# Adaptive average pooling: the last wait and its semaphore's clear, on GpSimd instead of SP

## The chip, the cores and the metric

The kernel runs on one core of one Trainium2 chip. A time is in device microseconds, lower being better, and comes from single executions of the program; the median of several is given with the lowest and highest. The profile is one such execution, recorded by the hardware profiler; its span goes from the first to the last instruction of the program.

Engines are named as in the profile: DVE is VectorE, ACT is ScalarE, POOL is GpSimd, SP is SyncE (no compute, it issues transfers and waits), PE is TensorE (idle in this kernel). A "q" behind a name (SPq, POOLq) is that engine's sequencer, which waits, signals and issues DMAs.

## The reference

```python
def setup_inputs():
    batch, channels, length = 32, 256, 4096
    output_size = 256
    ...

def reference(x, output_size):
    for i in range(output_size):
        start = int(i * length / output_size)
        end = int((i + 1) * length / output_size)
        result[:, :, i] = np.mean(x[:, :, start:end], axis=-1)
```

The input is 32 x 256 x 4096 float32, the output 32 x 256 x 256 float32. As 4096 is a multiple of 256, each output is the mean of its own 16 neighbours: 134 MB are read and 8.4 MB written.

## The kernel before

Batch and channel together give 8192 rows of 4096 values. They are spread over 128 partitions, four rows of a partition to a tile (`R = 4`), so a tile is 128 x 16384 float32 and there are 16 of them. The first 14 tiles belong to one set of rows and write into the buffer `res_many`; the last two, the tail, into `res_few`. Each of the two buffers is stored by one DMA of its own.

The loop (L65) runs over the 16 tiles with two input buffers. For each tile:

- L74: SP issues the load of the tile (`xin`).
- L77: POOL adds the second half of each window to its first half, for one half of the outputs.
- L82: DVE sums the 16 values of each window for the other half of the outputs.
- L85: DVE sums the 8 values left in the windows that POOL has halved.
- L88: ACT multiplies the tile's 1024 sums by 1/16, in place.

The store of `res_many` (L76) is issued by SP in the last pass of the loop, behind the last load; the store of `res_few` (L93) follows the loop. Both go through the helper `store`, so in the profile both have line L61. The helper keeps the two stores out of the framework's own bookkeeping of DMAs, and lets each of them add 16 to a semaphore of its own, `stored`.

The order within an engine is that of the program; between engines the framework puts waits on semaphores. At the end, `tc.compile()` (L97) puts in the closing sequence: SP waits for the framework's own DMA semaphores, all five engines pass a barrier (POOL leads it: it collects a signal from each of the others and then releases them), POOL clears the framework's semaphores (100 to 110) in one instruction, and a second barrier follows. These instructions have line L97 in the profile.

Only then come L98 and L99, which the change touches. The wait of L98 becomes part of the clear of L99: one instruction, which waits until `stored` (semaphore 99) is 32 and then sets it back to zero. It is the last instruction of the program; nothing of the program stands behind it on its engine. So the last store is under way while the closing sequence runs, and the wait for it comes after both barriers.

Of the kernel before, what the change touches and what calls it, by code (L numbers as in the profile page):

```python
# [1 line left out]

# [4 lines left out]


@with_exitstack
def kernel(  # L10
    ctx: ExitStack,
    tc: tile.TileContext,
    x: bass.AP,
    output_size: int,
    out: bass.AP,
):

    nc = tc.nc
    F32 = mybir.dt.float32
    X = mybir.AxisListType.X

    batch, channels, length = x.shape
    ob, oc, olen = out.shape
    assert ob == batch and oc == channels and olen == output_size
    assert length % output_size == 0
    window = length // output_size  # L30
    hw = window // 2
    inv_w = 1.0 / float(window)

    P = nc.NUM_PARTITIONS
    R = 4
    tail = 2
    rows = batch * channels
    assert rows % (P * R) == 0
    ntiles = rows // (P * R)
    head = ntiles - tail  # L40
    many = head * R
    few = tail * R
    cells = R * output_size
    m = cells // 2
    cols = R * length

    xr = x.rearrange("b c l -> (b c) l")
    orow = out.rearrange("b c o -> (b c) o")
    x_many = xr[0 : P * many, :].rearrange("(p r) l -> p (r l)", p=P, r=many)
    o_many = orow[0 : P * many, :].rearrange("(p r) o -> p (r o)", p=P, r=many)  # L50
    x_few = xr[P * many :, :].rearrange("(p r) l -> p (r l)", p=P, r=few)
    o_few = orow[P * many :, :].rearrange("(p r) o -> p (r o)", p=P, r=few)

    res_many = nc.alloc_sbuf_tensor("res_many", [P, head * cells], F32, align_bytes=256)
    res_few = nc.alloc_sbuf_tensor("res_few", [P, tail * cells], F32, align_bytes=256)
    inpool = ctx.enter_context(tc.tile_pool(name="inpool", bufs=2))

    stored = nc.alloc_semaphore("stored")

    def store(out, in_):  # L60
        ins = nc.sync.dma_start(out=out, in_=in_)  # L61
        tc.no_tile_sem_insts.add(ins.ins.name)
        ins.then_inc(stored, 16)

    for t in range(ntiles):  # L65
        k = t - head
        xin = inpool.tile([P, cells, window], F32, name="xin")
        if k < 0:
            res, base = res_many, t * cells
            src = x_many[:, t * cols : (t + 1) * cols]  # L70
        else:
            res, base = res_few, k * cells
            src = x_few[:, k * cols : (k + 1) * cols]
        nc.sync.dma_start(out=xin.rearrange("p o w -> p (o w)"), in_=src)  # L74
        if t == ntiles - 1:
            store(o_many, res_many[:, :])  # L76
        nc.gpsimd.tensor_add(  # L77
            out=xin[:, m:cells, 0:hw],
            in0=xin[:, m:cells, 0:hw],
            in1=xin[:, m:cells, hw:window],  # L80
        )
        nc.vector.reduce_sum(  # L82
            out=res[:, base : base + m], in_=xin[:, 0:m, :], axis=X
        )
        nc.vector.reduce_sum(  # L85
            out=res[:, base + m : base + cells], in_=xin[:, m:cells, 0:hw], axis=X
        )
        nc.scalar.mul(  # L88
            out=res[:, base : base + cells],
            in_=res[:, base : base + cells],  # L90
            mul=inv_w,
        )
    store(o_few, res_few[:, :])  # L93

    ctx.pop_all().close()
    tc.close()
    tc.compile()  # L97
    nc.sync.wait_ge(stored, 32)  # L98
    nc.sync.sem_clear(stored)  # L99


# [1 line left out]
_INS = ['x', 'output_size']  # L103
_OUTS = [((32, 256, 256), 'float32')]

_NUMBERS = {'output_size': 256}


# [26 lines left out]
```

## Time and profile before

| | |
|---|---|
| runs shown | median 333.56 us (333.36 to 333.82, 3 runs) |
| the profiled execution's own time | 333.14 us |
| its span | 331.8 us |
| DVE busy | 209.7 us (63%) |
| POOL busy | 139.7 us (42%) |
| ACT busy | 18.2 us (5%) |
| load of a tile, issue to landing | 25.4 us (median of 16) |
| read and written | 134.22 MB, 8.39 MB, at 430 GB/s over the span |

The execution's time is longer than the span, because the launch does things around the program that the span leaves out. Register, semaphore and DMA-issuing instructions don't count as busy, so SP, which does nothing else, has no busy time on the page; what it does is seen in the answers about one line, about SP's waits, and in the list of DMA issues. In an answer about one line, a row gives the engine, the operation and how often it came, then the lowest, median and highest duration in ns, and the start of the first and of the last one in us from the span's start. A row of SP's waits has what waited, what ended the wait, the time in total, the number of waits and the longest.

### The profile page before, as it was taken

How to read it: one execution, taken by the hardware profiler on the slowest of the kernel's cores; microseconds unless marked ns; L12 is line 12 of the kernel's file. 1: busy time of each engine (PE TensorE's matmuls, PEld its weight loads, DVE VectorE, ACT ScalarE, POOL GpSimd, SP SyncE). 2: the span in 40 equal slices, each digit the busy share in tenths (PEclk: the TensorE clock that was granted, in tenths of full speed). 3: DMA queues.
4: the chain of work that ended last, by engine and by line, in shares of the span. 5: the costliest groups of instructions: out<-in, count | busy, mean ns of one | idle time of the engine just before them, and what ended most of it. 6: DMA issues, size and time to landing. Idle time of an engine off the chain costs nothing.

```text
span 331.8 us, 159 instructions
## 1 busy us (share of the span) xinstructions
DVE 209.7 (63%) x32; ACT 18.2 (5%) x17; POOL 139.7 (42%) x20
## 2 busy tenths in 40 slices
DVE  0029396692939669392966939295693929569392
ACT  1000101001010100001010000101000010100001
POOL 0027090642709164270906437090643709063370
DMA  9898989989898998989899898989899898989998
GB/s 379 379 506 379 506 379 411 474 379 506 379 506 379 427 458 379 506 379 506 379 458 427 379 506 379 506 379 498 387 403 482 379 506 379 506 379 442 411 442 348
DMA packets 2592, 142.61 MB, mean 430 GB/s; under 512 B 288, under 2 KB 288, under 8 KB 288
## 3 DMA queue, kind: packets, MB, share of 16 engines
q1 hardware_dynamic: 2592, 142.61, 99.4%
HBM read 134.22 MB, written 8.39 MB: 430 GB/s over the span
## 4 chain that ended last, share of the span: by engine, by line
DMA 66%; POOL 18%; DVE 11%; POOLq 3%; issue 0%; ACT 0%; SPq 0%
DMA xin<-in_x_dram 66%; POOL xin L77 18%; DVE res_many L85 9%; POOLq L97 3%; DVE res_few L85 1%; ACT res_few L88 0%; SPq L74 0%; POOLq L77 0%
## 5 line engine op out<-in xcount | busy, mean ns | idle before, releaser
L77 POOL TENSOR_TENSOR xin<-xin 128x4096 f32<-128x4096 f32 x16 | 139.5, 8717 | 181.4 <-DMA xin<-in_x_dram 181.4
L82 DVE TENSOR_REDUCE res_many<-xin 128x512 f32<-128x8192 f32 x14 | 121.6, 8686 | 101.3 <-DMA xin<-in_x_dram 101.3
L85 DVE TENSOR_REDUCE res_many<-xin 128x512 f32<-128x4096 f32 x14 | 61.9, 4420 | 2.3 <-POOL xin L77 2.1
L88 ACT ACTIVATE res_many<-res_many 128x1024 f32<-128x1024 f32 x14 | 14.8, 1056 | 271.3 <-DVE res_many L85 271.3
L82 DVE TENSOR_REDUCE res_few<-xin 128x512 f32<-128x8192 f32 x2 | 17.4, 8686 | 12.1 <-DMA xin<-in_x_dram 12.1
L85 DVE TENSOR_REDUCE res_few<-xin 128x512 f32<-128x4096 f32 x2 | 8.8, 4420 | 0.3 <-POOL xin L77 0.3
L88 ACT ACTIVATE res_few<-res_few 128x1024 f32<-128x1024 f32 x2 | 2.1, 1056 | 36.6 <-DVE res_few L85 36.6
L88 ACT ACT_TABLE_LOAD x1 | 1.3, 1283 | 0.7 <-PEq L116 0.7
L116 POOL MEMSET const-float32-0.0<- 128x1 f32 x1 | 0.1, 98 | 0.2 <-issue 0.2
L116 POOL MEMSET const-uint8-127<- 128x1 uint8 x1 | 0.1, 102 | 0.0
L116 POOL MEMSET const-bfloat16-1.0<- 128x1 bf16 x1 | 0.1, 101 | 0.0
L116 POOL MEMSET const-float32-1.0<- 128x1 f32 x1 | 0.1, 99 | 0.0
## 6 DMA issues: line engine op xcount, KB each, us to landing
out_dram<-res_many SPq DMA_DIRECT2D x1, 7168.0 KB, 41.2
out_dram<-res_few SPq DMA_DIRECT2D x1, 1024.0 KB, 4.9
xin<-in_x_dram SPq DMA_DIRECT2D x16, 25.4
```

The source lines that it names most:

```text
L77: nc.gpsimd.tensor_add(out=xin[:, m:cells, 0:hw], in0=xin[:, m:cells, 0:hw], in1=xin[:, m:cells, hw:window],)
L82: nc.vector.reduce_sum(out=res[:, base : base + m], in_=xin[:, 0:m, :], axis=X)
L85: nc.vector.reduce_sum(out=res[:, base + m : base + cells], in_=xin[:, m:cells, 0:hw], axis=X)
L88: nc.scalar.mul(out=res[:, base : base + cells], in_=res[:, base : base + cells], mul=inv_w,)
L97: tc.compile()
L116: nc = _bacc.Bacc("TRN2", target_bir_lowering=False, num_devices=1)
```

## The change

The wait for `stored` and the clear of it are written for POOL's queue instead of SP's. Both stores are still issued by SP, with the same semaphore, and the place of the two lines in the program, behind `tc.compile()`, is the same.

```diff
     ctx.pop_all().close()
     tc.close()
     tc.compile()
-    nc.sync.wait_ge(stored, 32)
-    nc.sync.sem_clear(stored)
+    nc.gpsimd.wait_ge(stored, 32)
+    nc.gpsimd.sem_clear(stored)
```

## The prediction

> **What bounds the kernel now.** I read the page's first lines, then the chain of waits, then the DMA issues, then SP's own waits, and at last the lines that come after the work.
>
> ```profile
> DMA  9898989989898998989899898989899898989998
> q1 hardware_dynamic: 2592, 142.61, 99.4%
> DMA 66%; POOL 18%; DVE 11%; POOLq 3%; issue 0%; ACT 0%; SPq 0%
> ```
>
> The DMA engines are busy in nearly every slice, and one queue's packets fill 99.4% of sixteen engines' span. Loads set the pace up to the last tile. The change touches none of this: it edits two instructions behind the last barrier, so only the end counts. The end of the chain of waits:
>
> ```profile
> 312.55 8.75 POOLq L97
> 321.30 0.02 issue
> 321.33 4.43 DVE res_few L85
> 325.76 0.02 issue
> 325.78 1.06 ACT res_few L88
> ```
>
> The reader is to see that this chain stops at 325.78 + 1.06 = 326.84 us, while the span is 331.8 us. The missing 5.0 us are the last store and the wait for it, which the next views show: the timeline's last row, the issue's time to landing, and SP's wait.
>
> ```profile
> 326.86 0.34 SPq L61 DMA_DIRECT2D out_dram<-res_few  x1
> ```
>
> ```profile
> out_dram<-res_many SPq DMA_DIRECT2D x1, 7168.0 KB, 41.2
> out_dram<-res_few SPq DMA_DIRECT2D x1, 1024.0 KB, 4.9
> ```
>
> ```profile
> SPq L99 <- DMA out_dram<-res_few: 3.6, 1, 3.6
> ```
>
> SP issues the store of res_few at 326.86; it lands 4.9 us later, about 331.8. The earlier store started at 288.2 (its line's first start) and took 41.2, so it is done by 329.4 and does not decide. SP stands 3.6 us at L99, behind everything else of the program. The lines of L97 and L99 give the prices of what is moved:
>
> ```profile
> L97 POOLq EVENT_SEMAPHORE  x4: 17/17/17, 327.6 to 328.2; - x4
> L97 POOLq DRAIN  x3: 34/83/8809, 312.6 to 328.0; - x3
> L97 SPq DRAIN  x3: 7/7/7, 327.5 to 327.8; - x3
> L97 DVEq DRAIN  x2: 19/2236/4452, 321.3 to 327.9; - x2
> L97 POOLq EVENT_SEMAPHORE_RANGE_CLEAR  x1: 95/95/95, 327.9 to 327.9; - x1
> ```
>
> ```profile
> L99 SPq EVENT_SEMAPHORE_RANGE_CLEAR  x1: 25/25/25, 331.8 to 331.8; - x1
> ```
>
> **What lies behind the span.** The execution's own time is 333.14, the span 331.84: 1.30 us lie around it, and the trace's semaphore records show what. Semaphore 2 is in no line of the program; it is stepped nine times in each of two rounds after the program, and in the same rhythm just before it. The records, in us from the span's start:
>
> ```
> before the program  -0.371 -0.336 -0.298 -0.254 -0.231 -0.119 -0.081 -0.046  0.000
> first round after   328.503 328.537 328.742 328.786 331.962 332.006 332.044 332.078 332.126
> second round after  332.912 332.946 332.985 333.029 333.052 333.151 333.189 333.223 333.270
> ```
>
> Between the two later rounds all semaphores are reset in five blocks (207 to 255 from 332.083, 156 to 206 from 332.143, 105 to 155 from 332.180, 54 to 104 from 332.187, 3 to 53 from 332.341 to 332.688). I read a round as a barrier that goes through five engines and back: steps 1 to 4 on the way in, step 5 at the turn, 6 to 9 on the way out. SP sits at the turn: step 5 waits from 328.786 until 331.962, which is 0.122 after SP's clear ends (331.840), and the first instructions after the earlier round are SP 0.000, DVE 0.123, POOL 0.134, ACT 0.137, PE 0.315, the order of the way out. So the order in is PE, ACT, POOL, DVE, SP; ACT and POOL could be swapped, as their starts are 3 ns apart.
>
> The Trainium skill ("Runtime: NRT & Kernel Launch", "The ~15µs preamble/postamble breakdown") has such a barrier as a serpentine over five engines of 44 ns a hop, and 51 semaphores reset per engine; by its hop, a late third engine has two hops more in front of it than a late last one, an estimate of 0.088 us, where the records below give 0.121. It gives no longer way out for any one engine; without the exit difference used below the sum would be an estimate of about 0.12 (0.031 of later end and the 0.088) instead of 0.60.
>
> **The change, part by part.** Nothing before 328.2 moves: both instructions stand behind the last barrier of L97, whose POOL part ends at 328.180 and SP part at 328.223. The store's issue stays on SP's queue, at 326.86, before them. No DMA, tile or compute instruction is moved past a queue, and nothing of the program is queued behind the wait on POOL. POOL has 3.6 us to get to it.
>
> (1) SP loses its wait and clear. SP then is ready for the barrier at about 328.223 + 0.122 = 328.35, over 3 us early. This saves nothing by itself, since another engine is late in its place.
>
> (2) POOL's wake. The store's last increment is recorded at 331.798; SP's clear starts 17 ns later. POOL's barrier wait starts 23 ns after SP's drain (327.588 to 327.611). I take 331.821.
>
> (3) POOL's clear. Low end 25 ns (SP's clear of one semaphore), high end 95 (POOL's clear of the eleven of L97). In POOL's the first reset is recorded 22 ns after its start, and the last 26 ns before its end, so one semaphore should take some 50: POOL ends at 331.871. Ends: 331.846 to 331.916. SP ended at 331.840.
>
> (4) POOL's way out. POOL's last instruction now ends at 328.180 and step 3 comes at 328.742, 0.562 later. In the other rounds step 3 follows step 2 by 38 to 39 ns; here by 205, so the third engine itself was late. I take it to be POOL, because its drains (34 to 188 ns over L97 and the launch line L116, beside the one that waits for work) are longer than the other engines' (7 to 19). It is hidden now under the 3.6 us of L99; that cover goes away with the change. High end 0.562. Low end 0.122, which is what SP needs; PE needs 0.235 (328.268 to 328.503). I take 0.562, the row that is POOL's own: step 3 at 331.871 + 0.562 = 332.433. POOL's wait comes before this way out in its queue, so I see nothing that would let it run during the wait.
>
> (5) The rest of the barrier. With the third engine late, steps 4 to 9 remain; the second round has them at 44 + 23 + 99 + 38 + 34 + 47 = 285 ns. Step 9 comes at 332.718. Before it came at 332.126, which is four steps and 164 ns after step 5.
>
> Sum: 332.718 - 332.126 = +0.59, say **+0.60 us**; with both ends of (3), +0.57 to +0.64. The last block of resets starts behind step 9 and the second round behind its end (332.688 to 332.912), so all that follows moves by as much. On the profiled execution: 333.14 to 333.74. The runs shown have a median of 333.56 (333.36 to 333.82), 0.42 above it, since it was a short one; the same step there gives **334.15 us**. That is 0.18%. A measurement of this kernel tells about 0.2%, 0.67 us, from no change, so my forecast lies just below that line.
>
> **Rivals.**
> - *The way out is short or hidden* (0.28). The third engine was not POOL, or its 0.562 was something that passes during the 3.6 us wait, such as fetching what follows. Then POOL needs 0.122 to 0.235: 331.871 + 0.122 or 0.235 + 0.285 = 332.278 or 332.391, +0.15 to +0.27, so 333.7 to 333.8. For it: ACT and POOL can't be told apart by their starts. Against it: POOL's drains. If the time measured ends at the program's last instruction, only (2) and (3) are left, +0.03; the 1.30 us outside the span speak against that.
> - *Slower by over 0.2%: the clear itself is dear on POOL* (0.20). Place: between landing and way out. If clearing needs a drain of POOL as L97 has ahead of its clear (83 ns) and the full 95, POOL ends at 331.821 + 0.083 + 0.095 = 331.999, and the end moves by 0.72: 334.3. It decides from a POOL end of 331.94, which is 0.07 later than I take. For it: L97's three drains about the clear. Against it: this clear has no work of POOL to wait for and the program orders none.
> - *The change doesn't do what it says* (0.04): POOL's wait passes early, or the order of the ends does not count and freeing SP shortens its own resets. At most the stretch from the landing to step 5 would go, 331.962 - 331.798 = 0.16, so 333.4. Against it: the reset blocks of all five start behind step 5, SP's too.
>
> **How the numbers follow.** The forecast has 0.48. Since its +0.60 is 0.07 below the line and medians of runs move by 0.1 to 0.2, a third of it falls above the line: 0.16. With most of the third case that makes slower 0.35; faster gets 0.05, from the last case and from drift; the rest, 0.60, is within 0.2%. The range reaches from the short way out less the runs' spread (333.7 - 0.2 = 333.5) to the dear clear plus some of it (334.3 + 0.15 = 334.45).
>
> **What would show it.** The POOL clear of L99 in the lines: 25, 50 or 95 ns, and no drain at it. The span: 331.84 + 0.03 to 0.08. In the semaphore records step 3, not 5, is the one that waits for the store; its distance from POOL's last instruction is 0.56 (forecast) or under 0.25 (first rival). Then 285 ns to step 9, and a distance from span to execution time of 1.30 + 0.55 = 1.85 us. I am wrong if another step waits, if the second round does not follow step 9, or if the loads before 312 us differ.

## The result, and the profile after

The changed kernel took 334.08 us in the median (333.82 to 334.50, 19 runs), the kernel before 333.52 (333.23 to 334.03, 19 runs). The ratio is 1.0017, with a 95% interval of 1.0011 to 1.0024: slower by 0.56 us in the medians, or by 0.37 to 0.80 us. The forecast was +0.60, to 334.15.

The profiled execution of the changed kernel took 333.99 us, with a span of 332.16. Two views of it show the edit: SP's own waits, in which the row of L99 with its 3.6 us is gone (the two rows of L74, the loads, are left out here), and the answer about line L99, whose only instruction is now POOL's.

```profile
SPq L61 <- ACT res_few L88: 38.3, 1, 38.3
SPq L61 <- ACT res_many L88: 0.7, 1, 0.7
SPq L116 <- PEq L116: 0.7, 1, 0.7
SPq L97 <- PEq L97: 0.6, 2, 0.4
```

```profile
L99 POOLq EVENT_SEMAPHORE_RANGE_CLEAR  x1: 44/44/44, 332.1 to 332.1; - x1
```

The clear of one semaphore takes 44 ns on POOL and 25 on SP. The rows of L97 keep their durations (the 8.8 us drain, which waits for POOL's work, to 5 ns), and no drain has come in:

```profile
L97 POOLq EVENT_SEMAPHORE  x4: 17/17/17, 327.9 to 328.5; - x4
L97 POOLq DRAIN  x3: 34/83/8814, 312.8 to 328.3; - x3
L97 SPq DRAIN  x3: 7/7/7, 327.8 to 328.1; - x3
L97 POOLq EVENT_SEMAPHORE_RANGE_CLEAR  x1: 95/95/95, 328.2 to 328.2; - x1
```

Their starts are all some 0.3 us later than before. That is not the change's doing, as the end of the chain of waits, the timeline's last row and the issues show:

```profile
312.83 8.76 POOLq L97
321.59 0.02 issue
321.62 4.43 DVE res_few L85
326.05 0.02 issue
326.07 1.06 ACT res_few L88
```

```profile
327.15 0.34 SPq L61 DMA_DIRECT2D out_dram<-res_few  x1
```

```profile
out_dram<-res_many SPq DMA_DIRECT2D x1, 7168.0 KB, 41.2
out_dram<-res_few SPq DMA_DIRECT2D x1, 1024.0 KB, 4.9
```

ACT's last piece starts at 326.07 where it started at 325.78, the store follows 0.29 later, and it lands after the same 4.9 us. So 0.29 us had been lost before that, on the chain of loads and sums, where the two kernels do not differ. The span, 0.32 longer than before, therefore says almost nothing about the change: 0.29 of it is that chain, 0.026 is POOL's slower wake and clear. The cost stands outside the span, and is read from the semaphore records between the store's last increment and the last step of the launch's barrier:

```
                      store's last   first round, steps 1 to 9
                      increment
before (SP waits)     331.798        328.503 328.537 328.742 328.786 331.962 332.006 332.044 332.078 332.126
after (POOL waits)    332.090        328.791 328.826 332.685 332.729 332.752 332.851 332.890 332.924 332.971
```

Before, step 5 was the one that stood until the store had landed; now it is step 3. From the store's last increment to step 9 it took 332.126 - 331.798 = 0.328 us before and 332.971 - 332.090 = 0.881 after: +0.553 us. What follows has not changed: step 9 to the second round's last step takes 333.270 - 332.126 = 1.144 before and 334.116 - 332.971 = 1.145 after. The time of the execution moves with that last step: 333.270 - 333.14 = 0.13 before and 334.116 - 333.99 = 0.13 after (0.115 to 0.130 in all ten profiled executions of this document). So the 0.553 arrives whole in the time, and it fits the 0.56 of the medians.

The other runs show the same without a profile's records. Each run has its time and its span on record (the span to 0.1 us), and the time less the span does not hold what the loads did. It is 1.31 us on average before (1.25 to 1.35, 33 runs, taken with the experiments below) and 1.84 after (1.78 to 1.89, 19 runs): 0.53 more outside the span, where the records have 0.527.

### The profile page after: what moved, and what is told of

Same layout as the page of the kernel before. It is cut to its first block, busy times and chain, and to the rows that moved or that the text cites. A ratio compares the mean times of both kernels' runs of the same rounds, so it can differ in the third digit from the quotient of the medians.

```text
span 332.2 us, 159 instructions
## 1 busy us (share of the span) xinstructions
DVE 209.7 (63%) x32; ACT 18.2 (5%) x17; POOL 139.7 (42%) x20
## 4 chain that ended last, share of the span: by engine, by line
DMA 66%; POOL 18%; DVE 11%; POOLq 3%; issue 0%; ACT 0%; SPq 0%
DMA xin<-in_x_dram 66%; POOL xin L77 18%; DVE res_many L85 9%; POOLq L97 3%; DVE res_few L85 1%; ACT res_few L88 0%; SPq L74 0%; POOLq L77 0%
```

## The experiments

The theory: the engine that has the last wait pays four terms in turn: its wake (from the store's last increment to the start of its clear), its clear, its way out (from the end of its last instruction to its step of the first round), and the steps that are left behind its place, up to step 9. Rivals: any engine but SP pays the same; only the distance from SP matters; POOL's way out depends on what POOL has done, or on the clear.

**ACT, DVE and PE as the last engine.** One word of L98 and L99 is changed in each, `sync` to `scalar`, `vector` or `tensor`:

```diff
-    nc.sync.wait_ge(stored, 32)
-    nc.sync.sem_clear(stored)
+    nc.scalar.wait_ge(stored, 32)
+    nc.scalar.sem_clear(stored)
```

> The wait and the clear of stored are on ACT instead of SP. I count from the store's last increment to the ninth step of the first round behind the program: 0.328 us before, 0.881 with POOL. Theory (an engine costs its own way out plus the steps left behind its place): wake 0.02, clear 0.03, ACT's way out between 0.12 (SP's) and 0.31 (at most, from ACT's last instruction at 328.227 to step 2 at 328.537), and seven steps in 0.324: 0.50 to 0.69, so +0.17 to +0.36 us against before, and step 2 is the one that waits. Rival (any engine but SP pays about the same, since only SP sits at the turn): 0.88, +0.55 us.

> The wait and the clear of stored are on DVE instead of SP. Theory: wake 0.02, clear 0.04, DVE's way out between 0.12 and 0.55 (at most, from its last instruction at 328.237 to step 4 at 328.786), and five steps in 0.241: 0.42 to 0.85 from the store's last increment to step 9, so +0.09 to +0.52 us against before, nearer to the low end if POOL's way out is the odd one; step 4 is the one that waits. Rival (any engine but SP pays about the same): +0.55 us.

> The wait and the clear of stored are on PE instead of SP. Theory: wake 0.025, clear 0.06 (PE's event instructions take 51 ns where SP's take 17), PE's way out 0.235 (328.268 to 328.503) and all eight steps behind step 1 in 0.358: 0.68 from the store's last increment to step 9, so +0.35 us against before although PE stands furthest from the turn; step 1 is the one that waits. Rival (any engine but SP pays about the same): +0.55 us. Second rival (only the place counts, and a place further from the turn costs more): more than POOL's +0.55.

The answers about L99, of the kernels with ACT, DVE and PE in this order:

```profile
L99 ACTq EVENT_SEMAPHORE_RANGE_CLEAR  x1: 41/41/41, 332.2 to 332.2; - x1
```

```profile
L99 DVEq EVENT_SEMAPHORE_RANGE_CLEAR  x1: 55/55/55, 332.5 to 332.5; - x1
```

```profile
L99 PEldq EVENT_SEMAPHORE_RANGE_CLEAR  x1: 63/63/63, 332.2 to 332.2; - x1
```

The clear costs between 25 and 63 ns by engine, and POOL's 44 is in the middle. The first rounds, with the clear's end ahead of them:

```
last engine   clear ends   first round, steps 1 to 9
ACT           332.196      328.840 332.315 332.353 332.396 332.420 332.519 332.557 332.591 332.638
DVE           332.566      329.200 329.234 329.439 332.712 332.736 332.834 332.873 332.907 332.954
PE            332.220      332.459 332.493 332.532 332.576 332.599 332.697 332.737 332.771 332.817
```

Step 2 waits for ACT, step 4 for DVE and step 1 for PE, which with SP's step 5 and POOL's step 3 settles the order on the way in: PE, ACT, POOL, DVE, SP. The four terms in us, each read from the records of its own profiled execution (the last column takes POOL's median against the 333.52 of its own comparison, the others against 333.39):

| last engine | wake | clear | way out | steps left | sum | more than SP | medians: more than before |
|---|---|---|---|---|---|---|---|
| SP (before) | 0.017 | 0.025 | 0.122 | 0.164 (4) | 0.328 | | |
| DVE | 0.029 | 0.055 | 0.146 | 0.242 (5) | 0.472 | 0.144 | 0.26 |
| ACT | 0.021 | 0.041 | 0.119 | 0.323 (7) | 0.504 | 0.176 | 0.23 |
| PE | 0.029 | 0.063 | 0.239 | 0.358 (8) | 0.689 | 0.361 | 0.46 |
| POOL (after) | 0.024 | 0.044 | 0.527 | 0.286 (6) | 0.881 | 0.553 | 0.56 |

The theory's bounds hold for all three (0.50 to 0.69, 0.42 to 0.85, and 0.68 at a point); PE's is met to 0.01. That any engine but SP pays the same falls: the sums lie between 0.472 and 0.881. That only the distance from SP counts falls too: PE stands furthest and is 0.19 us cheaper than POOL. The times agree as far as they can tell. Against a median of 333.39 before, ACT's 333.62 has a ratio of 1.0007 (0.9998 to 1.0016) and DVE's 333.65 of 1.0006 (0.9998 to 1.0015), so by time alone neither is shown to be slower; PE's 333.85 has 1.0012 (1.0003 to 1.0021). The times less the spans do tell them apart from SP's 1.25 to 1.35: 1.36 to 1.45 with DVE, 1.42 to 1.51 with ACT and 1.57 to 1.66 with PE (11 runs each). On average that is 0.09, 0.15 and 0.31 us more than before, where the way out and the steps left give 0.10, 0.16 and 0.31.

With PE last, the whole round of eight hops, from step 1 to step 9, runs without a stop, in 0.358 us. The Trainium skill ("Runtime: NRT & Kernel Launch", "The ~15µs preamble/postamble breakdown") gives some 355 ns, 44 ns a hop, for this serpentine ahead of a program. The traces agree with the total, here and in the round just ahead of the program (0.370 to 0.372), though not with an even hop: the steps here are 23 to 46 ns apart, and steps 5 and 6 are 98.

That one long hop is part of SP's advantage. When SP is the late one, step 6 follows step 5 by 43 or 44 ns, and in the four other cases by 98 or 99. So SP's four steps cost 0.164 us and not some 0.218: 0.054 us of what SP saves does not come from the number of steps alone.

ACT's round shows one thing more. POOL's last instruction there ends at 328.517, 3.8 us before step 2, and step 3 follows step 2 by 38 ns. So POOL's way out costs nothing when it begins early enough; among the engines tried it is paid where POOL has the last wait.

**A drain behind the clear.**

```diff
     nc.gpsimd.wait_ge(stored, 32)
     nc.gpsimd.sem_clear(stored)
+    nc.gpsimd.drain()
```

> As changed (wait and clear on POOL), with a drain of POOL behind the clear. Theory (POOL's way out of 0.53 us is a fixed cost that runs behind its last instruction): the drain comes on top with 34 to 83 ns and a gap of some 30, so 0.95 to 1.0 us from the store's last increment to step 9, +0.06 to +0.11 against the changed kernel and +0.62 to +0.67 against before. Rival (the way out is for the most part one draining of POOL's cores, which the added drain does ahead of it): the way out shrinks by about what the drain takes, and the sum stays at 0.88, +0.55 against before.

```profile
L100 POOLq DRAIN  x1: 34/34/34, 332.3 to 332.3; - x1
```

The drain takes 34 ns and begins 29 ns behind the clear. Step 3 comes 0.526 behind the drain's end (332.355 to 332.881), where it came 0.527 behind the clear's, and the sum is 0.941: the drain lies on top in full. The way out is not something that this drain does ahead. I had expected 0.95 to 1.0, so the sum came 0.009 under the range; the 0.060 over the changed kernel is at its low end. The time is 334.01 against 333.39 (ratio 1.0021, 1.0012 to 1.0030), which is +0.62, also at the low end.

**POOL without work.** DVE sums all of a window and POOL's addition is gone, once with the wait on SP and once with it on POOL:

```diff
-        nc.gpsimd.tensor_add(
-            out=xin[:, m:cells, 0:hw],
...
-            out=res[:, base + m : base + cells], in_=xin[:, m:cells, 0:hw], axis=X
+        nc.vector.reduce_sum(
+            out=res[:, base : base + cells], in_=xin[:, :, :], axis=X
         )
```

> POOL computes nothing: DVE sums all 16 values of every window in one instruction a tile, and the wait and the clear stay on SP. It is the control for the next run. DVE's 17.4 us a tile stay under a load's 25; behind the last load DVE now takes 17.4 instead of 13.3, so both theories expect some +4 us against before, and 0.33 us from the store's last increment to step 9.

> As the run before, with the wait and the clear on POOL, which still computes nothing. Theory (POOL's way out of 0.53 us is its own, whatever it did before): 0.88 us from the store's last increment to step 9, and 0.55 us more than with the wait on SP. Rival (the way out closes what POOL's work has opened, its tensor instructions and the pool configuration ahead of them): the way out falls to SP's 0.12 or PE's 0.24, so 0.47 to 0.59 to step 9 and +0.15 to +0.27 us.

From the page of the kernel with the wait on SP (busy time of each engine):

```profile
DVE 275.5 (78%) x16; ACT 18.2 (5%) x17; POOL 0.2 (0%) x4
```

and a piece of its chain of waits:

```profile
59.04 24.11 DMA xin<-in_x_dram
83.16 0.02 issue
83.18 17.23 DVE res_many L77
```

The sums from the store's last increment to step 9 are 0.328 with SP and 0.880 with POOL, whose way out is 0.527 (352.091 to 352.618), the same as behind sixteen additions. So it does not close anything that POOL's additions have opened. The medians, 354.07 and 354.63, differ by 0.56, but the runs of each spread over 3 to 5 us, so this difference alone proves nothing. The records do, and so do the times less the spans: 1.27 to 1.32 with SP and 1.79 to 1.87 with POOL (6 runs each).

My expectation of the time itself, +4 us, was wrong: it is +20.7 (354.07 against 333.39). I had counted the longer sum once, behind the last load, and taken the rest to be hidden under the loads. The chain shows that it isn't: a load that needs a buffer waits for the sum that frees it, so every second tile's sum stands on the chain, 24.11 + 17.23 = 41.3 us for two tiles. Before, the chain had 25.48 + 8.73 + 4.43 = 38.6 for the same two: the sum was 4.1 shorter and the load 1.4 longer. The chain holds eight sums, the first one and seven that follow a load of their own, so this pair of rows puts the difference at 4.1 + 7 x 2.7 = 23 us; in the profiled execution the last sum ends 22.0 later (347.76 for 325.76), and the store lands 3.8 us after its issue for 4.9, which gives 1.1 back.

**No clear.** The line of the clear is left out, with the wait on SP and with it on POOL. The semaphore is left at 32 for the launch's own reset, which the records have at 332.550 and 333.066.

```diff
     nc.gpsimd.wait_ge(stored, 32)
-    nc.gpsimd.sem_clear(stored)
```

> As before, without the clear of stored; SP only waits (the launch resets all semaphores behind the program). Theory: the wait alone takes 17 to 28 ns on SP in place of the clear's 25, so nothing: 0.32 to 0.33 us from the store's last increment to step 9, within 0.01 of before. Rival (a clear holds its engine on the way out): up to 0.1 us less.

> As changed, without the clear: POOL only waits. Theory: the clear's 44 ns become the 17 of an event instruction and the way out stays at 0.53 to 0.56, so 0.85 to 0.88 us from the store's last increment to step 9 and +0.52 to +0.55 us against before. Rival (it is the clear on POOL that is dear, its end being recorded too early): the way out falls under 0.25 and the sum to 0.55 us, +0.2 against before.

The answers about L98, with the wait on SP and on POOL:

```profile
L98 SPq EVENT_SEMAPHORE  x1: 17/17/17, 332.0 to 332.0; - x1
```

```profile
L98 POOLq EVENT_SEMAPHORE  x1: 17/17/17, 331.9 to 331.9; - x1
```

The sums are 0.315 with SP and 0.857 with POOL, and POOL's way out is 0.531 (331.955 to 332.486). The clear is worth 13 ns on SP and 24 on POOL in the sum, where its row is 8 and 27 ns longer than the bare wait's, and has no part in POOL's way out. POOL's sum is as expected; SP's came 0.005 under the expected 0.32 to 0.33. Times: 333.38 against 333.39 with SP (ratio 1.0000, 0.9991 to 1.0008), 333.94 against 333.39 with POOL (1.0017, 1.0008 to 1.0026). No version here beats the kernel before: SP has the smallest sum of the five engines, and its 0.013 without the clear can't be seen in the time.

## Why the prediction was right

Step by step, against the changed kernel's records:

1. SP freed early saves nothing: right. Steps 1 and 2 come at 328.8, and step 3 holds the round.
2. POOL's wake: 23 ns forecast, 24 measured (332.090 to 332.114).
3. POOL's clear: 50 ns taken from how the eleven resets of L97 lie within its 95; 44 measured. No drain at it, so the second rival, a dear clear, is gone.
4. The way out: 0.562 forecast, 0.527 measured. This is the term that was over by most, 0.035 us. That it is POOL's, which I chose for its longer drains, was right; the reason was weak, since the drain run shows that an added drain takes nothing off the way out. What carried the choice was the late step 3 alone, and by the starts that I had read it could have been ACT's step, whose own way out is 0.119. That POOL was the one is in part luck.
5. The rest of the round: 285 ns forecast, 286 measured.

The sum of these was 0.59 and is 0.553; the clear's 0.006 and the way out's 0.035 are nearly all of the difference. The step from the profiled execution to the median held as well: +0.56 in the medians of 19 runs. The forecast of 334.15 lies 0.07 over the measured 334.08, about half from the step (0.59 for 0.56) and half from the three runs before, whose 333.56 became 333.52 with 19.

One of my own signs of being wrong came up: the chain before 312 us differs, 312.83 for 312.55, and the span grew by 0.32 where I had said 0.03 to 0.08. It does not touch the mechanism, since the edit stands behind that chain and the times less the spans leave it out: 1.84 us on average, for the 1.85 that I had forecast.

The first rival had two forms. That the third engine was not POOL falls with step 3, which now waits for POOL. That the way out passes during the wait is refuted, except perhaps for the 0.035: POOL stood at the wait for 3.6 us (328.469 to 332.114) and still took 0.527 behind it. The third rival, in which freeing SP shortens its resets, is refuted: from step 9 on, the two executions agree to 2 ns, and POOL's clear starts 24 ns behind the store's last increment, so its wait did not pass early. I gave 0.60 to a change within 0.2% and 0.35 to more; it came at 0.17%, with an interval of 0.11% to 0.24% that reaches over the line, so the 0.07 us by which the forecast lay below it could not have been known to suffice.

What POOL does in its 0.53 us stays open. The profile has nothing of POOL's between its last instruction and step 3. The runs exclude its additions, the clear, and anything that one drain would do ahead. Why it was 0.562 in the kernel before, 0.035 longer, is open too: there POOL's last instruction was the second barrier's release and no wait stood between, and the run with SP last and POOL idle has the same 0.56 (350.171 to 350.732). Whether fetching what follows is behind the 0.035 was not tried.

## What to carry to other kernels

The last wait of a program is best put on the engine whose way out is short and which stands last on the way into the launch's closing barrier; here that is SP, and each other engine costs 0.14 to 0.55 us more. That was measured on this program and a variant of it alone. The span hardly shows it, as it ends with the program's last instruction: to judge an edit at the end, follow the records from the event that both versions share (here the store's last increment) to the end of what is timed, or subtract the span from the time, run by run. And the difference of two spans holds what the chain of loads happened to do in the two executions, here 0.29 us, as much as the edit.

## What the runs showed that I had not expected

- POOL needs 0.526 to 0.531 us from its last instruction to its step of the launch's barrier in all four profiled kernels where it goes last, busy or idle, with or without a clear; the other engines need 0.119 to 0.239.
- The clear of one semaphore takes 25 ns on SP, 41 on ACT, 44 on POOL, 55 on DVE and 63 on PE, and the wake behind the last increment 17 to 29 ns.
- With SP as the late engine step 6 follows step 5 by 43 or 44 ns, with any other by 98 or 99.
- A sum longer by 4.1 us a tile cost 20.7 us in a kernel whose DMA engines had looked nearly full, since with two buffers each load from the third on waits for a sum.
